# A transposed input in two halves of the tokens for the opening stage of a two-layer attention encoder

## The chip, the cores and the metric

The kernel runs on one core of one Trainium2 chip. The metric is the device time of one execution in microseconds; the profile comes from one profiled execution on the chip. Times of instructions are read from its trace.

## What is computed

A two-layer encoder over 1024 tokens of 1024 features, in float32. Each layer normalises x, scales and shifts it feature by feature (the modulation, computed from a vector c by a product with `ada_w`), projects it, runs attention and adds the gated result to x. Layer 0 joins latent attention (queries and keys go through narrow latents of 384 and 256 features, each with a norm of its own) with stick-breaking attention; layer 1 is differential attention. The change concerns the start of layer 0 as far as the latents `cq` and `ckv`.

```python
def rms_norm(x, g, eps=NORM_EPS):
    xf = x.astype(jnp.float32)
    y = xf * lax.rsqrt(jnp.mean(xf * xf, axis=-1, keepdims=True) + eps)
    return (y * g.astype(jnp.float32)).astype(x.dtype)
...
def layer_ab(h, pos, w_in, q_norm_g, kv_norm_g, w_uq, w_ukv, w_out):
    B, S, _ = h.shape
    proj = h @ w_in
    cuts = np.cumsum([MLA_Q_LORA, MLA_KV_LORA, MLA_ROPE, SB_W, SB_W, SB_W]).tolist()
    cq, ckv, kr, q_sb, k_sb, v_sb, z = jnp.split(proj, cuts, axis=-1)
    q = (rms_norm(cq, q_norm_g) @ w_uq).reshape(B, S, MLA_HEADS, MLA_NOPE + MLA_ROPE)
    ...
    kv = (rms_norm(ckv, kv_norm_g) @ w_ukv).reshape(B, S, MLA_HEADS, MLA_NOPE + MLA_V)
    ...
    o_mla = mla_attention(q, k, kv[..., MLA_NOPE:]).reshape(B, S, MLA_HEADS * MLA_V)
    o_sb = stick_breaking_attention(q_sb.reshape(shp), k_sb.reshape(shp), v_sb.reshape(shp)).reshape(B, S, SB_W)
    y = jnp.concatenate([o_mla, o_sb], axis=-1) * jax.nn.silu(z)
    return y @ w_out
...
    c_act = jax.nn.silu(c)
    for i in range(DEPTH):
        mod = c_act @ ada_w[i] + ada_b[i]
        shift, scale, gate = jnp.split(mod, 3, axis=-1)
        h = rms_norm(x, norm_g[i]) * (1.0 + scale[:, None, :]) + shift[:, None, :]
        ...
        x = x + gate[:, None, :] * out
    return rms_norm(x, final_g)
```

## The kernel before

Every matrix product is done as three: each operand is split into a high part, rounded to 12 bits, and an exact rest, and `mm3` (lines 172 to 175) adds high x high, high x low and low x high into one PSUM bank. A block of weights is 128 columns wide; `wprep` (line 164) loads it into the tile `w_st`, ScalarE casts the high part and VectorE or GpSimd subtracts the rest (`split`, `sub`, lines 153 to 162). `dense_fm` (line 177) multiplies one block with the 8 feature blocks of the tokens, in two halves of 512 tokens, 24 products each.

The order of work is that of a scheduler: instructions are written in a program order, it places them on the engines when its model finds them ready, and every engine then runs its own list in that order. SP's list holds all DMA issues. Tiles with one tag share a fixed number of slots, so a tile can wait for the release of another.

The opening (lines 496 to 728) makes the modulated, transposed tokens hT: 8 feature blocks of 128 rows by 1024 tokens, as high and low parts (`h0h`, `h0l`). x comes in 8 tiles of 128 tokens by 1024 features. ScalarE or VectorE square and sum each row (lines 523 and 526), `rstd_cols` (line 188) makes the inverse root in thirteen small VectorE instructions, and each tile is scaled in one pass (lines 532, 534). For feature block k, `ada_block` (line 538) computes shift and scale: eight VectorE instructions over a 1 MB tile of `ada_k` (lines 542 and 544, tile `ack`), sums over partitions on TensorE (line 547), two tiny instructions (lines 548, 549). Then TensorE transposes the eight 128 x 128 pieces of x (line 554), and `modulate` (line 237) lets ScalarE scale and shift a bank of four into `hf` and cast the high part, while GpSimd or VectorE subtracts the low one.

The first three latent blocks run feature by feature as hT comes, for all tokens, in six PSUM banks; the fourth and fifth follow whole. `latent` (line 612) evacuates each bank with a square on ScalarE (line 620), a cast times a gain (line 621) and a subtraction on VectorE (line 622), stores both parts to DRAM for later, and makes the norm of the three query blocks and of the two key blocks by column sums (`row_sums`, line 230). Behind them come the relative position rows, the rotary tables, the rotated shared key (block 21), four blocks of the gate z, and, by `more` (line 606), in pieces queued behind the last x subtraction (`ready`) and the last store of the first three latents (`behind`), the modulation sweeps for layer 1 and the gates (`ada_sweep`, line 472). Then the stick-breaking heads begin.

## Time and profile before

| | |
|---|---|
| Median of 3 runs | 1491.65 us (1491.1 to 1492.06) |
| Span of the profiled execution | 1489.6 us |
| TensorE products busy | 1394.9 us, 94% of the span |
| VectorE busy | 956.8 us, 64% |
| ScalarE busy | 670.5 us, 45% |
| GpSimd busy | 446.2 us, 30% |

Busy shares are averages over stages. The profile gives them in forty slices too, and the trace can be asked for a stretch, for one engine in order of time, or for groups of instructions by line. A row in order of time has the start, the duration, the engine, the line and the operation with its output and inputs; several equal instructions in a row are merged (x4). In square brackets stands the idle time before it and what released it. A product's duration overlaps with the next one's, so the spacing of starts tells its cost.

### The profile page before, as it was taken

Reading aid. Unit: us, or ns where it says so; the run is one execution under the profiler, and the core shown is the slowest. Engines: PE = TensorE matmul, PEld = TensorE weight load, DVE = VectorE, ACT = ScalarE, POOL = GpSimd, SP = SyncE. Lnnn points to the kernel's source line nnn. Section 1 sums busy time; section 2 is a strip of 40 time slices with the busy share of each in tenths; the row PEclk is TensorE's granted clock in tenths of the full one; section 3 lists DMA queues with packets and bytes.
Section 4 is the critical chain, followed back from the end, with each engine's and each line's share of the span. In section 5 each row is a group of like instructions: output and inputs, shape, how many; then the busy total and the mean of one; then the engine's idle time right before and its main releaser. Section 6 shows DMA issues by size and latency. Waiting matters only on the chain.

```text
span 1489.6 us, 20993 instructions
## 1 busy us (share of the span) xinstructions
PE 1394.9 (94%) x7328; PEld 1160.7 (78%) x7328; DVE 956.8 (64%) x2155; ACT 670.5 (45%) x1368; POOL 446.2 (30%) x509
## 2 busy tenths in 40 slices
PE   3899999999998899999879899999999999997797
...
GB/s 375 67 261 382 206 77 75 49 90 50 75 69 186 36 188 213 136 123 100 215 136 268 29 108 48 86 85 114 71 100 64 92 64 114 78 111 179 82 201 93
DMA packets 109640, 189.85 MB, mean 127 GB/s; under 512 B 8736, under 2 KB 70040, under 8 KB 107488
## 3 DMA queue, kind: packets, MB, share of 16 engines
...
## 4 chain that ended last, share of the span: by engine, by line
PE 40%; DVE 5%; DMA 4%; issue 1%; POOL 1%; ACT 1%; SPq 0%; DVEq 0%; ACTq 0%; POOLq 0%
PE psd L173 8%; PE psd L175 8%; PE psd L174 8%; PE sc L294 4%; PE pv L328 3%; PE sc L173 2%; PE sc L174 2%; PE sc L175 2%; DMA y_hi<-yh_d 1%; DMA w_st<-in_wo_dram 1%; PE pv L234 1%; PE tr L308 1%; PE tr L309 1%; PE tr L310 1%; DVE g L1029 1%
## 5 line engine op out<-in xcount | busy, mean ns | idle before, releaser
L154 POOL TENSOR_TENSOR w_lo<-w_st,w_hi 128x1024 fp32r<-128x1024 f32 (+2 forms) x63 | 153.6, 2440 | 370.7 <-ACT w_hi L159 370.4
L154 DVE TENSOR_TENSOR pt_l<-tr,pt_h 128x512 fp32r<-128x512 f32 (+1 forms) x240 | 148.8, 630 | 104.9 <-ACT pt_h L159 97.4
L159 ACT CAST pt_h<-tr 128x512 fp32r<-128x512 f32 (+1 forms) x240 | 126.2, 547 | 147.0 <-PE tr L310 136.1
L175 PE MATMUL psd<-h1h,w_lo 128*128 128x512 f32 x448 | 177.0, 395 | 0.0
L174 PE MATMUL psd<-h1l,w_hi 128*128 128x512 f32 x448 | 176.2, 393 | 0.0
L173 PE MATMUL psd<-h1h,w_hi 128*128 128x512 f32 x448 | 176.1, 393 | 0.0
L294 PE MATMUL sc<-qk_k,qk_a 128*128 128x512 f32 (+2 forms) x288 | 104.8, 369 | 3.6 <-ACT g L747 1.3
L173 PE MATMUL psd<-h0h,w_hi 128*128 128x512 f32 x264 | 106.7, 404 | 0.0
L174 PE MATMUL psd<-h0l,w_hi 128*128 128x512 f32 x264 | 105.6, 400 | 0.0
L175 PE MATMUL psd<-h0h,w_lo 128*128 128x512 f32 x264 | 105.2, 398 | 0.0
L294 PE MATMUL sc<-qk_k,qk_b 128*128 128x512 f32 (+2 forms) x288 | 98.5, 349 | 0.0
L1029 DVE CUSTOM_DVE_ANT_0 g<-sc,tz 128x512 f32<-128x512 f32 (+3 forms) x128 | 72.1, 585 | 40.1 <-PE sc L294 33.7
L159 ACT CAST w_hi<-w_st 128x1024 fp32r<-128x1024 f32 x56 | 58.9, 1052 | 86.4 <-PE sc L174 36.2
L174 PEld LDWEIGHTS psd<-h1l,w_hi 128*128 128x128 f32 x448 | 84.2, 188 | 17.1
L175 PEld LDWEIGHTS psd<-h1h,w_lo 128*128 128x128 f32 x448 | 84.2, 188 | 16.1
L173 PEld LDWEIGHTS psd<-h1h,w_hi 128*128 128x128 f32 x448 | 84.2, 188 | 16.1
L328 PE MATMUL pv<-pt_l,vt 128*128 128x256 f32 x320 | 88.7, 303 | 8.2 <-DVE pt_l L154 7.4
L1035 ACT ACTIVATE g<-g,st 128x640 f32<-128x640 f32 (+3 forms) x64 | 63.4, 990 | 67.8 <-DVE st L1034 63.1
L328 PE MATMUL pv<-pt_h,vt 128*128 128x256 f32 x320 | 89.5, 296 | 3.3 <-POOL pt_h L314 1.7
L749 DVE TENSOR_TENSOR_SCAN g<-g 128x640 f32<-128x640 f32 (+3 forms) x32 | 68.7, 2148 | 14.7 <-ACT g L746 14.6
L328 PEld LDWEIGHTS pv<-pt_l,vt 128*128 128x128 f32 x320 | 62.0, 194 | 12.0 <-issue 4.7
L328 PEld LDWEIGHTS pv<-pt_h,vt 128*128 128x128 f32 x320 | 61.8, 193 | 9.5 <-DVE ot L418 2.7
...
## 6 DMA issues: line engine op xcount, KB each, us to landing
...
```

The source lines that it names most:

```text
L154: return (nc.vector if eng == "vec" else nc.gpsimd).tensor_tensor(out_, x_, y_, op=ALU.subtract)
L159: nc.scalar.copy(hi, src)
L173: mm(ps, sh, mh, start=start, stop=False)
L174: mm(ps, sh, ml, start=False, stop=False)
L175: mm(ps, sl, mh, start=False, stop=stop)
L234: mm(ps[:, t:t + 1], tile_of(t), ones, start=True, stop=True)
L294: mm(ps[:, :nn], st[:, q], mv[:, lo_:lo_ + nn], start=m == 0, stop=not diag and m == len(pairs) - 1)
L308: nc.tensor.transpose(tr[:, P:256], pb[:, (2 * j + 1) * P:(2 * j + 2) * P], identf)
L328: mm(dst, st, tt[w][:, m * 256:m * 256 + 256], start=j == 0 and m == 0 and x == 0, stop=j == n - 1 and m == 1 and x == len(ps_) - 1)
L749: nc.vector.tensor_tensor_scan(ur, ur, ur, 1.0, op0=ALU.mult, op1=ALU.bypass)
L1029: nc.vector.tensor_tensor_reduce(e_[:, sl], ps, tz[:, S - L + sl.start:S - L + sl.stop], op0=ALU.add, op1=ALU.max, scale=1.0, scalar=-3e38 ...
L1035: nc.scalar.activation(e_[:, :L], e_[:, :L], AF.Exp, scale=0.125, bias=st[:, 2 + c:3 + c], accum_out=lst[:, c1:c1 + 1] if c == 0 else st[: ...
```

## The change

x is handed over transposed and cut into two halves of 512 tokens (`xt`: for each half four tiles with two feature blocks each). `x_norm` squares the eight feature blocks of a half on ScalarE, adds them up (VectorE for the first half, GpSimd for the second), takes column sums on TensorE, the inverse root, and spreads it over the partitions by four scaled identities and products (`cols_bc`) into a tile `rbx`. `x_mod` multiplies a feature block by it, lets ScalarE scale, shift and cast it, and subtracts the low part; the multiplication and the subtraction are VectorE's for features 0 and 1 of the first half and for even features of the second, GpSimd's otherwise. The transposes of x go. Five latent blocks instead of three run feature by feature, on the first half alone, in five banks; then their banks are evacuated in half-width tiles, the second half is normalised and modulated, and the five blocks run on it one after the other. The norms of the latents follow at the end. All five split weights stay on the chip meanwhile. Feature block 0 of the modulation is summed by TensorE instead of VectorE; the first two weight blocks have their low parts from VectorE, the others from GpSimd. `ready` is now the last subtraction of the second half, `behind` the last store of all five latents.

The diff, without removed comments and docstrings and without renamed tiles further down:

```diff
-SC = "avavavvv"
-LOK = lambda k, g: k in (0, 7)
-WLO = ("vec", "pool")
+WLO = ("vec", "vec", "pool", "pool", "pool")
...
-    X_TAGS = [("lsq0", 1), ("lsq1", 1), ("lsq2", 1), ("zb", 2), ("zb", 2), ("lat_h", 2), ("lat_h", 2), ("lat_l", 2)]
...
         def ada_load(k):
             ada_st[k] = a0.tile([P, KC, 256], F32, name="ada_st", tag="ld", bufs=NLD)
             dma(ada_st[k].rearrange("p r c -> p (r c)"), a["ada_k"][k])
-            return ada_st[k]
-        xts = []
-        junka = a0.tile([P, 2, D], F32, name="junka", tag="acc")
-        for g in range(2):
-            ss = a0.tile([P, 4], F32, name="ss", tag="ss", bufs=2)
+        def wide(name, tag):
+            return a0.tile([P, S], F32, name=name, tag=tag, bufs=4)
+        def x_load(half):
+            ts = []
             for j in range(4):
-                t = 4 * g + j
-                tag, bufs = X_TAGS[t]
-                xt = a0.tile([P, D], F32, name="xt", tag=tag, bufs=bufs)
-                dma(xt, a["x"][t * P:t * P + P, :])
-                if j % 2:
-                    junk = a0.tile([P, D], F32, name="junk", tag="junk")
-                    nc.vector.tensor_tensor_reduce(junk, xt, xt, op0=ALU.mult, op1=ALU.add, scale=1.0, scalar=0.0,
-                                                   accum_out=ss[:, j:j + 1])
-                else:
-                    nc.scalar.activation(junka[:, 0, :], xt, AF.Square, accum_out=ss[:, j:j + 1])
-                xts.append(xt)
-            rs = rstd_cols(a0, ss, 4, 1.0 / D, 1e-6, "rc")
-            for j in range(4):
-                xt = xts[4 * g + j]
-                if SC[4 * g + j] == "a":
-                    nc.scalar.activation(xt, xt, AF.Copy, scale=rs[:, j:j + 1])
-                else:
-                    nc.vector.tensor_scalar(xt, xt, rs[:, j:j + 1], None, op0=ALU.mult)
-            if g == 0:
-                ada_load(0)
+                t_ = wide("xt", "ab"[half])
+                dma(t_, a["xt"][half, j])
+                ts.append(t_)
+            return [ts[k // 2][:, k % 2 * 512:k % 2 * 512 + 512] for k in range(KC)]
+        def x_norm(half, xk):
+            add = nc.vector if half == 0 else nc.gpsimd
+            acc = a0.tile([P, 512], F32, name="sqa", tag="sqa", bufs=1)
+            for k in range(KC):
+                sq = acc if k == 0 else a0.tile([P, 512], F32, name="sq", tag="hf", bufs=2)
+                nc.scalar.activation(sq, xk[k], AF.Square)
+                if k:
+                    add.tensor_tensor(acc, acc, sq, op=ALU.add)
+            ss = row_sums(lambda t: acc[:, t * P:t * P + P], 4, v_bank)
+            r = rstd_cols(a0, ss, 4, 1.0 / D, 1e-6, "rc")
+            bc = cols_bc(acc, r, v_bank)
+            rb = a0.tile([P, 512], F32, name="rbx", tag="rbx", bufs=1)
+            nc.vector.tensor_copy(rb, bc)
+            return rb
         def ada_block(k):
-            st = ada_st[k] if k in ada_st else ada_load(k)
-            ac = a0.tile([P, 256], F32, name="ack", tag="ack", bufs=2)
-            nc.vector.tensor_scalar(ac, st[:, 0, :], c_act[:, 0:1], None, op0=ALU.mult)
-            for r in range(1, KC):
-                nc.vector.scalar_tensor_tensor(ac, st[:, r, :], c_act[:, r:r + 1], ac, op0=ALU.mult, op1=ALU.add)
+            st = ada_st[k]
             ps = t_bank()
-            for n in range(2):
-                mm(ps[:, n:n + 1], ac[:, n * P:n * P + P], ones, start=True, stop=True)
+            if k == 0:
+                for n in range(2):
+                    for r in range(KC):
+                        mm(ps[:, n:n + 1], st[:, r, n * P:n * P + P], c_act[:, r:r + 1], start=r == 0, stop=r == KC - 1)
+            else:
+                ac = a0.tile([P, 256], F32, name="ack", tag="ack", bufs=2)
+                nc.vector.tensor_scalar(ac, st[:, 0, :], c_act[:, 0:1], None, op0=ALU.mult)
+                for r in range(1, KC):
+                    nc.vector.scalar_tensor_tensor(ac, st[:, r, :], c_act[:, r:r + 1], ac, op0=ALU.mult, op1=ALU.add)
+                for n in range(2):
+                    mm(ps[:, n:n + 1], ac[:, n * P:n * P + P], ones, start=True, stop=True)
             nc.vector.tensor_tensor(modc[0][:, k::8], ps[:, 0:2], adab[:, k:16:8], op=ALU.add)
             nc.vector.scalar_tensor_tensor(gsc[0][:, k:k + 1], modc[0][:, 8 + k:9 + k], 1.0, ng[:, k:k + 1],
                                            op0=ALU.add, op1=ALU.mult)
-            for g in range(2):
-                tr = t_bank()
-                for j in range(4):
-                    nc.tensor.transpose(tr[:, j * P:(j + 1) * P], xts[4 * g + j][:, k * P:(k + 1) * P], identf)
-                last = modulate(a0, hT, 0, k, slice(g * 512, g * 512 + 512), tr, "act", "vec" if LOK(k, g) else "pool")
-            return last
+        def x_mod(half, k, xk, rb):
+            sl = slice(half * 512, half * 512 + 512)
+            vec = (k < 2) if half == 0 else (k % 2 == 0)
+            (nc.vector if vec else nc.gpsimd).tensor_tensor(xk, xk, rb, op=ALU.mult)
+            nc.scalar.activation(xk, xk, AF.Identity, scale=gsc[0][:, k:k + 1], bias=modc[0][:, k:k + 1])
+            return split(hT[k][0][:, sl], hT[k][1][:, sl], xk, "act", "vec" if vec else "pool")
+        in_a0 = lambda tag, bufs: (lambda t_: (lambda name: t_[:, 0 if name == "w_hi" else 1, :]))(
+            a0.tile([P, 2, 1024], F32R, name="wl", tag=tag, bufs=bufs))
+        def w_load(b):
+            alloc = None if b < 2 else in_a0("acc", 1) if b == 2 else in_a0("ld", NLD)
+            return wprep(a["w0"][16 + b], eng_lo=WLO[b], alloc=alloc)
+        x0 = x_load(0)
+        ada_load(0)
+        wl = [w_load(0), w_load(1)]
+        rb0 = x_norm(0, x0)
         ada_block(0)
-        wq3 = [wprep(a["w0"][16 + b], eng_lo=WLO[b]) for b in range(2)]
-        w3 = a0.tile([P, 2, 1024], F32R, name="w3", tag="acc")
-        wq3.append(wprep(a["w0"][18], alloc=lambda name: w3[:, 0 if name == "w_hi" else 1, :]))
-        first = [[s_bank(), s_bank()], [s_bank(), d_bank()], [d_bank(), v_bank()]]
+        wl.append(w_load(2))
+        ada_load(1)
+        wl += [w_load(3), w_load(4)]
+        for k in (2, 3):
+            ada_load(k)
+        wlk = [tuple(t_.rearrange("p (k c) -> p k c", c=P) for t_ in w) for w in wl]
+        fb = [s_bank(), s_bank(), s_bank(), d_bank(), d_bank()]
+        x_mod(0, 0, x0[0], rb0)
         for k in range(KC):
             if k + 1 < KC:
-                ready = ada_block(k + 1)
-            for b in range(3):
-                wh, wl = (t.rearrange("p (k c) -> p k c", c=P) for t in wq3[b])
-                for half in range(2):
-                    sl = slice(half * 512, half * 512 + 512)
-                    mm3(first[b][half], wh[:, k, :], wl[:, k, :], hT[k][0][:, sl], hT[k][1][:, sl], k == 0, k == KC - 1)
-        w4 = a0.tile([P, 2, 1024], F32R, name="w4", tag="ld", bufs=NLD)
-        wk = [wprep(a["w0"][19], alloc=lambda name: w4[:, 0 if name == "w_hi" else 1, :])]
+                ada_block(k + 1)
+                x_mod(0, k + 1, x0[k + 1], rb0)
+                if k + 4 < KC:
+                    ada_load(k + 4)
+            if k == 0:
+                x1 = x_load(1)
+            for b in range(5):
+                mm3(fb[b], wlk[b][0][:, k, :], wlk[b][1][:, k, :], hT[k][0][:, :512], hT[k][1][:, :512], k == 0, k == KC - 1)
+        sqt = {}
+        def latent_evac(b, half, ps):
+            sl = slice(half * 512, half * 512 + 512)
+            if b % 2 == 0:
+                sqt[half, b // 2] = wide("lsq", "ab"[half])
+            gain, hi_d, lo_d, j = (qg, cqh_d, cql_d, b) if b < 3 else (kvg, ckh_d, ckl_d, b - 3)
+            nc.scalar.activation(sqt[half, b // 2][:, b % 2 * 512:b % 2 * 512 + 512], ps, AF.Square)
+            lh = a0.tile([P, 512], F32R, name="lat_h", tag="lat_h", bufs=2)
+            ll = a0.tile([P, 512], F32R, name="lat_l", tag="lat_l", bufs=2)
+            nc.scalar.activation(lh, ps, AF.Copy, scale=gain[:, j:j + 1])
+            nc.vector.scalar_tensor_tensor(ll, ps, gain[:, j:j + 1], lh.bitcast(F32), op0=ALU.mult, op1=ALU.subtract)
+            dma(hi_d[j][:, sl], lh)
+            return dma(lo_d[j][:, sl], ll)
+        for b in range(5):
+            latent_evac(b, 0, fb[b])
+        rb1 = x_norm(1, x1)
+        for k in range(KC):
+            ready = x_mod(1, k, x1[k], rb1)
+        for b in range(5):
+            ps = (s_bank, d_bank)[b % 2]()
+            for k in range(KC):
+                mm3(ps, wlk[b][0][:, k, :], wlk[b][1][:, k, :], hT[k][0][:, 512:], hT[k][1][:, 512:], k == 0, k == KC - 1)
+            behind = latent_evac(b, 1, ps)
...
-        def latent(nblk, w_first, gain, hi_d, lo_d, row_d, banks=None):
-            tags = [("lsq0", 1), ("lsq1", 1), ("lsq2", 1)] if banks else [("zb", 2)] * 2
-            sq = [a0.tile([P, S], F32, name="lsq", tag=tag, bufs=bufs) for tag, bufs in tags]
-            for b in range(nblk):
-                lh = a0.tile([P, S], F32R, name="lat_h", tag="lat_h", bufs=2)
-                ll = a0.tile([P, S], F32R, name="lat_l", tag="lat_l", bufs=2)
-                def evac(ps, half, sl):
-                    nc.scalar.activation(sq[b][:, sl], ps, AF.Square)
-                    nc.scalar.activation(lh[:, sl], ps, AF.Copy, scale=gain[:, b:b + 1])
-                    nc.vector.scalar_tensor_tensor(ll[:, sl], ps, gain[:, b:b + 1], lh[:, sl].bitcast(F32),
-                                                   op0=ALU.mult, op1=ALU.subtract)
-                if banks:
-                    for half in range(2):
-                        evac(banks[b][half], half, slice(half * 512, half * 512 + 512))
-                else:
-                    dense_fm(wk.pop() if wk else wprep(a["w0"][w_first + b]), hT, evac, s_bank)
-                dma(hi_d[b], lh)
-                stored = dma(lo_d[b], ll)
-            for x_ in sq[1:]:
-                nc.gpsimd.tensor_tensor(sq[0], sq[0], x_, op=ALU.add)
-            ss = row_sums(lambda t: sq[0][:, t * P:t * P + P], NT, v_bank)
-            r = rstd_cols(a0, ss, NT, 1.0 / (nblk * P), 1e-6, "rl")
+        def latent_norm(b0, n, row_d):
+            part = lambda half, b: sqt[half, b // 2][:, b % 2 * 512:b % 2 * 512 + 512]
+            for half in range(2):
+                for b in range(b0 + 1, b0 + n):
+                    nc.gpsimd.tensor_tensor(part(half, b0), part(half, b0), part(half, b), op=ALU.add)
+            ss = row_sums(lambda t: part(t // 4, b0)[:, t % 4 * P:t % 4 * P + P], NT, v_bank)
+            r = rstd_cols(a0, ss, NT, 1.0 / (n * P), 1e-6, "rl")
             row_out(a0, r, NT, row_d, v_bank)
-            return stored
-        krt = a0.tile([P, S], F32, name="krt", tag="lat_h", bufs=2)
+        krt = wide("krt", "b")
...
-        behind = latent(3, 16, qg, cqh_d, cql_d, rq_d, first)
+        latent_norm(0, 3, rq_d)
+        latent_norm(3, 2, rkv_d)
...
-        rqb = a0.tile([P, S], F32, name="rqb", tag="lsq2", bufs=1)
+        rqb = wide("rqb", "b")
         dma(rqb, row_bc(rq_d, P))
-        latent(2, 19, kvg, ckh_d, ckl_d, rkv_d)
         more(3)
-        te = a0.tile([P, S], F32, name="te", tag="lsq0")
+        te = wide("te", "a")
         nc.vector.tensor_copy(te[0:64], rqb[0:64])
         nc.vector.tensor_mul(te[64:128], rqb[64:128], cs[64:128])
         dma(tq_d[0], te)
-        to = a0.tile([P, S], F32, name="to", tag="lsq1")
+        to = wide("to", "a")
         nc.vector.tensor_mul(to[0:64], rqb[0:64], cs[0:64])
         nc.vector.tensor_copy(to[64:128], rqb[64:128])
         dma(tq_d[1], to)
...
-        "x": f["x"][0], "pos": f["pos_offset"].reshape(1, 1), "tab": f["rel_bias_table"],
+        "x": f["x"][0], "xt": f["x"][0].T.reshape(4, 2, P, 2, 512).transpose(3, 0, 2, 1, 4).reshape(2, 4, P, 1024),
+        "pos": f["pos_offset"].reshape(1, 1), "tab": f["rel_bias_table"],
```

## Rows read from the trace of the kernel before

**Rows 1.** The page's busy tenths of TensorE, forty slices of 37.2 us.
```profile
PE   3899999999998899999879899999999999997797
```

**Rows 2.** Stretches: PE, PEld, DVE, ACT, POOL busy us (instructions), clock, DMA share, GB/s.
```profile
40.00:45.00 5.00, 1.34 (x6) 0.75 (x4) 5.00 (x4) 1.87 (x3) 5.00 (x3) 0.88 0.01 5
...
50.00:60.00 10.00, 10.00 (x51) 8.30 (x50) 9.09 (x13) 3.95 (x7) 5.30 (x4) 0.97 0.34 107
...
70.00:80.00 10.00, 10.00 (x53) 8.04 (x51) 3.74 (x9) 6.24 (x10) 2.57 (x2) 1.00 0.06 14
```

**Rows 3.** TensorE in order of time, 25 to 52 us: start us, us, engine, line, what.
```profile
25.18 0.80 PE L173 MATMUL sc<-h0h,w_hi 128*128 128x512 f32 x1 [4.00 <-ACT h0h L159]
...
45.88 0.98 PE L547 MATMUL tr<-ones_sq,ack 128*128 128x1 f32 x4 [4.54 <-DVE ack L544]
...
49.32 0.63 PE L174 MATMUL sc<-h0l,w_hi 128*128 128x512 f32 x1
...
49.74 0.63 PE L175 MATMUL sc<-h0h,w_lo 128*128 128x512 f32 x1
...
51.75 0.40 PE L173 MATMUL psd<-h0h,w 128*128 128x512 f32 x1
...
51.98 0.40 PE L174 MATMUL psd<-h0l,w 128*128 128x512 f32 x1
```

**Rows 4.** TensorE in order of time, 80 to 109 us.
```profile
80.07 0.81 PE L585 MATMUL tr<-oh,tab 32*8 32x384 f32 x2
...
99.25 1.84 PE L234 MATMUL pv<-ones_sq,lsq 128*128 128x1 f32 x16
...
108.56 0.39 PE L175 MATMUL sc<-h0h,w_lo 128*128 128x512 f32 x1
```

**Rows 5.** VectorE in order of time, 27 to 60 us.
```profile
27.93 0.35 DVE L542 TENSOR_SCALAR ack<-ada_st,c_act 128x256 f32<-128x256 f32 x1
...
28.19 0.88 DVE L544 SCALAR_TENSOR_TENSOR ack<-ada_st,c_act,ack 128x256 f32<-128x256 f32 x2
...
28.98 0.68 DVE L154 TENSOR_TENSOR h0l<-hf,h0h 128x512 fp32r<-128x512 f32 x1
...
29.58 4.56 DVE L544 SCALAR_TENSOR_TENSOR ack<-ada_st,c_act,ack 128x256 f32<-128x256 f32 x11
...
38.02 9.14 DVE L544 SCALAR_TENSOR_TENSOR ack<-ada_st,c_act,ack 128x256 f32<-128x256 f32 x9
...
55.76 3.61 DVE L544 SCALAR_TENSOR_TENSOR ack<-ada_st,c_act,ack 128x256 f32<-128x256 f32 x7
```

**Rows 6.** GpSimd in order of time, 36 to 63 us.
```profile
36.68 2.65 POOL L154 TENSOR_TENSOR h0l<-hf,h0h 128x512 fp32r<-128x512 f32 x2 [13.37 <-ACT h0h L159]
...
42.54 2.52 POOL L154 TENSOR_TENSOR w<-w_st,w 128x1024 fp32r<-128x1024 f32 x1
...
52.21 2.90 POOL L154 TENSOR_TENSOR h0l<-hf,h0h 128x512 fp32r<-128x512 f32 x2
...
59.80 2.53 POOL L154 TENSOR_TENSOR h0l<-hf,h0h 128x512 fp32r<-128x512 f32 x2 [4.70 <-ACT h0h L159]
```

**Rows 7.** TensorE in order of time: a transpose of x.
```profile
57.09 1.04 PE L554 MATMUL tr<-identf,xt 128*128 128x128 f32 x8
```

**Rows 8.** VectorE in order of time: its square of the fourth x tile.
```profile
9.12 1.23 DVE L523 CUSTOM_DVE_ANT_0 junk<-xt 128x1024 f32<-128x1024 f32 x1 [1.43 <-DMA xt<-in_x_dram]
```

**Rows 9.** ScalarE by line and form, 0 to 250 us: count | busy us, mean ns | idle before.
```profile
L239 ACT ACTIVATE hf<-tr,modc,gsc 128x512 f32<-128x512 f32 x16 | 12.2, 777 | 33.4 <-DVE gsc L549 20.9 <-PE tr L554 10.8 <-POOL h0l L154 1.7
...
L159 ACT CAST h0h<-hf 128x512 fp32r<-128x512 f32 x16 | 9.7, 622 | 0.3
```

**Rows 10.** VectorE in order of time: the first and last of thirteen root steps.
```profile
140.02 0.15 DVE L192 TENSOR_SCALAR rlh<-pv 128x8 f32<-128x8 f32 x1
...
142.22 0.17 DVE L203 SCALAR_TENSOR_TENSOR rlr<-rlt,rlr 128x8 f32<-128x8 f32 x1
```

**Rows 11.** SP's queue in order of time: the first issues of the later modulation.
```profile
93.65 10.02 SPq L80 DMA_DIRECT2D ada_st<-in_ada_w_dram  x10
```

6 lines of the change are left out of this document (3 added, 3 removed).

## Prediction

> **What bounds the kernel now.** I began with the busy shares in forty slices: TensorE stands at eight or nine tenths nearly everywhere, and at three in the first slice of 37 us [rows 1]. So a change in the opening is worth what it does to the moment from which TensorE no longer starves, plus or minus the TensorE work behind it. The table of stretches gives that moment: from 40 to 45 us TensorE is busy for 1.34 us of 5, from 50 us on it is busy all the time [rows 2]. The order of TensorE's instructions says the same: the first product of the latent blocks starts at 25.18, there is a wait of 4.54 us before 45.88 with DVE's accumulation (`ack`) as the releaser, and from 51.75 products start every 0.23 us [rows 3]. The last of the 240 products of the five latent blocks starts at 108.56 and so ends at about 109.0 us; sixteen row sums of the queries' norm and the small table products lie ahead of it [rows 4]. I take **109.0 us** as the mark: whatever the change does to it, the saturated work behind it moves with it.
>
> What starves TensorE is not DMA, which is idle from 40 to 45 us (5 GB/s) [rows 2]. It is VectorE and GpSimd together. Alone, VectorE runs eleven accumulations in 4.56 us, 0.407 us each; beside GpSimd nine take 9.14 us [rows 5], and GpSimd at that time runs one subtraction after another [rows 6]. To see whether the two exclude each other I added up the 31.4 us from 27.93 to 59.37, in which VectorE is never idle: 41 accumulations of 0.407 (16.7), five first steps of 0.26 (1.3), one subtraction of 0.60, eight tiny instructions (0.9), and on GpSimd six half-width subtractions of 1.27 and two full ones of 2.45 (12.5) [rows 5, 6]. That is 32.0 us of work in 31.4 us. So in this stage instructions of the two engines on on-chip tiles add up as if they ran on one engine; I call it the shared budget.
>
> The Trainium skill states the same in "SBUF — State Buffer", section "SBUF: two separate sides": VectorE instructions with two SBUF inputs, or in a two-port mode, and GpSimd's exclude each other for a whole instruction; it speaks against the change. It leaves out instructions with one input in PSUM, such as the `lat_l` subtraction. No run here separates those; if they counted, the first half's five would add an estimated 3.8 us to the sum below, and by the page they add nothing.
>
> **The change, part by part.**
>
> *x arrives transposed, the 64 transposes go.* Eight transposes take some 0.8 us at the fast spacing [rows 7]; 36 of the 64 lie after 50 us, where TensorE is the limit, so about 3.5 us of its work goes there. The rest lay in starved time and is worth nothing. The loads stay eight of 512 KB on the same queue: no change.
>
> *Start.* The fourth x tile is in at 9.1 us [rows 8], and it is now all that the first half needs. Then: two squares on ScalarE, 1.2 (by the 0.62 us of a 512-column pass [rows 9]); one addition, 0.6 (the spacing of a 512-column subtraction [rows 5]); four column sums on a slow TensorE, 1.0 (the row at 45.88 [rows 3]); thirteen small instructions for the root, 2.4 [rows 10]; spreading the columns over the partitions, which the trace of before does not show: at least four small steps, 0.8, at most 2.0 with four products between them, I take 1.5 as the steps pipeline; a copy, 0.6. That is 16.4 us; one weight subtraction (1.2) falls into it, so **17.5 us**. The scaling, the affine pass (0.78) and the cast (0.62) [rows 9] put the first product near 20, five microseconds before the old one. That alone brings nothing if the stage behind it is slower.
>
> *The shared budget from 17.5 us until the second half can begin.* VectorE: seven accumulation blocks (block 0 goes to TensorE, where it runs in idle time) of 0.26 + 7 x 0.407 = 3.11, 21.8 us; scaling and subtraction of features 0 and 1, 4 x 0.60 = 2.4. GpSimd: the low halves of three weight blocks, 3 x 2.45 = 7.4; scaling and subtraction of six features, 12 x 1.27 = 15.2; the seven additions of the second half's norm, 8.9. Sum 55.7, so it is through at **73.2 us**. Before, the normalisation was one pass over the wide tile by ScalarE or VectorE; now every feature block pays a multiplication by the row of norms, most of them on the slower engine. Within this budget the order hardly matters: additions early delay the accumulations, additions late delay the second half.
>
> *TensorE meanwhile.* Five blocks on one half are 15 products a feature: 3.5 us at 0.23, 6.3 at 0.42 [rows 3]. The budget gives a feature about every 7 us, so TensorE keeps up at either clock and is idle for about half of the stage. The first half ends near 76 us.
>
> *The change of halves.* The second half's norm goes through column sums, root, spreading and copy once more and then scaling, affine pass and cast: 1.0 + 2.4 + 1.5 + 0.6 + 0.6 + 0.8 + 0.6 = 7.5, so the first product of the second half starts at **80.7 us**. Nothing else is ready for TensorE but the table products. Its 120 products take 27.6 us. The idle time ahead of them resembles the 4.54 us before 45.88, after which products were 0.42 us apart until about 50 us, the 1.2 GHz level [rows 3]; that costs ten products 0.19 us each, 1.9. Two things can hold up the second half's features: ScalarE has 8 x 1.4 us for them and stands behind the first half's evacuation, which now has two half-width `lat_h` tiles that wait for their stores; and their share of the budget is 15 us for eight, 1.9 us each, against 3.5 us that five interleaved blocks or 0.7 us that a single block needs. That is 0 to 4 us; I take 1.5. The sixteen row sums, 1.7 [rows 4]. Together 80.7 + 27.6 + 1.9 + 1.5 + 1.7 = 113.4, and 1.0 for table products and row sums that do not fit into idle time: **114.4 us against 109.0, 5.4 us later**.
>
> *Behind the mark.* `more` queues the sixteen tiles of layer 1's modulation on SP behind the last latent store; before, that is 93.65 [rows 11], because three blocks were through early; now it follows all five, near 115. Half of the latent stores have left by then, on an idle DMA. The sums over partitions of these sweeps stand in TensorE's order among the z blocks; I take the delay at zero, covered by three to four blocks of products (11 us each), and 8 us if the cover is gone. The key norm, now beside the query norm, costs what it did.
>
> Sum: profiled span 1489.6 + 5.4 = 1495.0. The median of the runs lies 2.05 us above the span, so **1497 us**.
>
> **Rivals.**
> 1. *The forecast*: a slower opening by the shared budget, 1493 to 1502: 0.47.
> 2. *Ideal interleaving.* The second half's norm and first features are worked off within the first half, so that products run on without a hole: first half through at 73.2 + 3.5 = 76.7, second at 104.3, row sums 106.0, 3.0 us earlier: 1488.7. For it: the budget is the same in any order. Against it: GpSimd has to pass 23 us of work that stands earlier in the program, and the hole at the change of halves is a chain of small steps. Up to 1493 it is no measurable change: 0.22.
> 3. *The budget is only partly shared* (faster). If half of GpSimd's 31.5 us runs beside VectorE, the budget ends at 57.5, the second half starts at 65 and the mark is at 98.7: 10 us earlier, 1481. With none of it shared GpSimd's 31.5 us alone set the stage, 49.0 us, and the mark is at 90.2: 1473. It decides from 10 us of overlap on. For it: VectorE's instructions of this stage with a PSUM input, and tiny ones, may pass. Against it: the 32.0 in 31.4 us. 0.18, most of it at the near end.
> 4. *The modulation of layer 1 comes late.* The second sweep's sums hold TensorE: another 8 us, 1505. For it: they start 20 us later while TensorE is only 5 later. Against it: half of the latent stores no longer compete with them for DMA. 0.13.
>
> That the transposes are not really gone, or x is loaded twice, the diff excludes.
>
> **How the numbers follow.** A measurement of this kernel tells about 0.2%, 3 us, from no change. The predicted time is that of the first case. Faster by more than that: case 3 and the best part of case 2, 0.23. Within: the rest of case 2 and the near edge of case 1, 0.22. Slower: 0.55. The range for eight in ten runs from 1482, the near end of case 3, to 1506, case 4; it leaves out a budget that is not shared at all and a double delay.
>
> **What would show it.** Right: no transposes of x; the first product near 20 us; VectorE's accumulations slow (1 us and more) wherever GpSimd is busy, between 18 and 70 us; TensorE about half idle until 75 us; a hole of some 5 us before the first product on the second half near 81 us, at the low clock behind it; the last latent product near 113. Wrong: accumulations of 0.4 us beside a busy GpSimd, a last feature of the first half before 60 us, or a mark before 105 us. If the mark is where I put it but the end is not, the loss or gain lies in the modulation sweeps or in the clock of the z blocks.

## The result and the profile after

The changed kernel takes 1528.96 us (median of 4 runs, 1526.02 to 1533.41) against 1491.86 us (4 runs, 1491.1 to 1492.73) on the same chip: 2.5% slower, ratio 1.0247, 95% interval 1.0225 to 1.0268. The forecast had the sign and not the size: 5.4 us later were forecast, 37.1 came. The profiled execution spans 1526.9 us against 1489.6, 37.3 more.

The page after, busy tenths of TensorE and its granted clock in forty slices of 38.2 us; TensorE answers to [rows 1]:

```profile
PE   4689799999999889999888899999999999998897
...
PEclk9689799999999999999999999999999999998899
```

The weak stretch no longer ends with the first slice: slices two and three (38 to 115 us) stand at 6 and 8, the fifth (153 to 191 us) at 7, where before there were eights and nines. So two stages lost time. The table of stretches after (TensorE, its weight loads, VectorE, ScalarE, GpSimd busy us; clock; DMA share; GB/s), against [rows 2]:

```profile
30.00:40.00 10.00, 5.21 (x17) 3.33 (x16) 1.21 (x1) 1.74 (x3) 10.00 (x7) 0.89 0.16 48
...
50.00:60.00 10.00, 5.13 (x17) 4.40 (x18) 9.93 (x33) 1.43 (x2) 1.30 (x1) 0.50 0.98 368
...
70.00:80.00 10.00, 4.34 (x10) 3.13 (x10) 10.00 (x14) 6.83 (x11) 8.12 (x5) 0.66 0.00 1
80.00:90.00 10.00, 4.50 (x13) 3.75 (x14) 7.95 (x16) 4.69 (x9) 2.67 (x2) 0.60 0.00 0
...
150.00:160.00 10.00, 3.11 (x13) 2.23 (x12) 10.00 (x21) 0.00 (x0) 10.00 (x1) 0.86 0.99 401
...
180.00:190.00 10.00, 7.16 (x21) 5.75 (x22) 9.96 (x17) 0.00 (x0) 0.00 (x0) 0.66 0.93 385
```

From 30 to 40 us VectorE works 1.21 us of 10 and GpSimd all 10; from 70 to 80 us both are busy (10.00 and 8.12), from 80 to 90 us still VectorE (7.95), and TensorE works less than half of the time at a granted clock of 0.66 and 0.60; from 150 to 160 us both are busy all the time and TensorE works 3.11 us.

To size the two stages I use two marks. The first is the prediction's: the end of the last latent product with the sixteen row sums of the queries' norm. The second is ScalarE's first cast of the stick-breaking stage. TensorE after, in order of time (answering to [rows 4]), then that cast before and after:

```profile
131.56 0.40 PE L173 MATMUL sc<-h0h,wl 128*128 128x512 f32 x1
131.80 1.84 PE L232 MATMUL pv<-ones_sq,lsq 128*128 128x1 f32 x16
133.50 0.47 PE L171 MATMUL sc<-h0h,w_hi 128*128 128x512 f32 x1
```

```profile
L159 ACT CAST qk_a<-psd x5: 576/587/634, 187.0 to 245.9; 128x512 fp32r<-128x512 f32 x5
```

```profile
L157 ACT CAST qk_a<-psd x3: 576/586/587, 223.4 to 247.3; 128x512 fp32r<-128x512 f32 x3
```

| stage | before | after | difference |
|---|---|---|---|
| to the mark | 109.0 | 133.5 | +24.5 |
| mark to first cast | 78.0 | 89.9 | +11.9 |
| rest of the span | 1302.6 | 1303.5 | +0.9 |

**The opening.** SP's queue, then VectorE, GpSimd and TensorE after, in order of time:

```profile
15.87 24.11 SPq L78 DMA_DIRECT2D w_st<-in_w_dram  x4
40.03 2.00 SPq L78 DMA_DIRECT2D ada_st<-in_ada_k_dram  x4
```

```profile
22.28 0.69 DVE L532 COPY rbx<-pv 128x512 f32<-128x512 f32 x1 [0.32 <-PE pv L225]
...
23.28 3.43 DVE L558 TENSOR_TENSOR xt<-xt,rbx 128x512 f32<-128x512 f32 x2
...
46.43 0.84 DVE L545 TENSOR_SCALAR ack<-ada_st,c_act 128x256 f32<-128x256 f32 x1 [15.03 <-DMA ada_st<-in_ada_k_dram]
...
68.50 6.79 DVE L558 TENSOR_TENSOR xt<-xt,rbx 128x512 f32<-128x512 f32 x4
...
87.43 0.48 DVE L547 SCALAR_TENSOR_TENSOR ack<-ada_st,c_act,ack 128x256 f32<-128x256 f32 x1
...
93.18 0.16 DVE L550 TENSOR_TENSOR modc<-tr,smalls 128x2 f32<-128x2 f32 x1 [5.19 <-PE tr L549]
```

```profile
24.45 9.33 POOL L558 TENSOR_TENSOR xt<-xt,rbx 128x512 f32<-128x512 f32 x6
33.74 1.26 POOL L527 TENSOR_TENSOR sqa<-sqa,sq 128x512 f32<-128x512 f32 x1
34.96 4.67 POOL L152 TENSOR_TENSOR wl<-w_st,wl 128x1024 fp32r<-128x1024 f32 x2
...
44.48 3.98 POOL L527 TENSOR_TENSOR sqa<-sqa,sq 128x512 f32<-128x512 f32 x3
...
66.84 6.23 POOL L558 TENSOR_TENSOR xt<-xt,rbx 128x512 f32<-128x512 f32 x4 [2.67 <-DVE rbx L532]
```

```profile
13.36 6.96 PE L542 MATMUL tr<-c_act,ada_st 128*128 128x1 f32 x32
20.19 2.05 PE L225 MATMUL pv<-sqa,ones_sq 128*128 128x128 f32 x8
...
26.97 1.22 PE L171 MATMUL sc<-h0h,w_hi 128*128 128x512 f32 x2 [2.53 <-ACT h0h L157]
...
74.80 0.79 PE L172 MATMUL sc<-h0l,w_hi 128*128 128x512 f32 x1 [5.50 <-POOL h0l L152]
85.50 0.98 PE L549 MATMUL tr<-ones_sq,ack 128*128 128x1 f32 x4 [6.37 <-DVE ack L547]
103.93 0.50 PE L171 MATMUL sc<-h0h,w_hi 128*128 128x512 f32 x1 [1.01 <-DVE lat_l L605]
```

SP's queue stands from 15.87 to 40.0 us at four weight tiles: the staging tile `w_st` has two buffers, and one is freed only by GpSimd's low half at 34.96, behind six multiplications and two additions. Modulation tiles 2 to 5 stand behind them in the queue, so VectorE is idle for 15.03 us, while GpSimd works without a pause (22.99 to 48.46). Afterwards the two engines hold each other up: a multiplication that takes 0.6 us alone (e6 below) takes 1.7 (6.79 for four). These four and GpSimd's four at 66.84 are the second half's, and they stand in the lists ahead of what the first half's last features still need. The second half's first product starts at 103.93, with hardly a wait.

**Behind the mark.** TensorE, GpSimd and VectorE after (the first step of a norm's root, the first sweep steps, ten more):

```profile
158.96 0.79 PE L171 MATMUL sc<-h0h,w_hi 128*128 128x512 f32 x1 [6.89 <-DVE krt L668]
182.84 0.80 PE L171 MATMUL sc<-h0h,w_hi 128*128 128x512 f32 x1 [4.97 <-DVE zb L249]
```

```profile
145.81 14.72 POOL L152 TENSOR_TENSOR w_lo<-w_st,w_hi 128x1024 fp32r<-128x1024 f32 x1 [11.80 <-ACT w_hi L157]
167.97 2.35 POOL L152 TENSOR_TENSOR w_lo<-w_st,w_hi 128x1024 fp32r<-128x1024 f32 x1
```

```profile
133.93 0.15 DVE L190 TENSOR_SCALAR rlh<-pv 128x8 f32<-128x8 f32 x1
...
139.62 0.88 DVE L476 TENSOR_SCALAR acc<-ada_st,c_act 128x512 f32<-128x512 f32 x2 [3.31 <-DMA ada_st<-in_ada_w_dram]
...
143.80 6.69 DVE L478 SCALAR_TENSOR_TENSOR acc<-ada_st,c_act,acc 128x512 f32<-128x512 f32 x10
```

VectorE before, the same two first steps, and TensorE's wait for `krt` from mark to first cast (us in total, times, longest):

```profile
101.29 0.16 DVE L192 TENSOR_SCALAR rlh<-pv 128x8 f32<-128x8 f32 x1
102.13 0.88 DVE L478 TENSOR_SCALAR acc<-ada_st,c_act 128x512 f32<-128x512 f32 x2 [0.69 <-DMA ada_st<-in_ada_w_dram]
```

```profile
PE sc L173 <- DVE krt L642: 0.4, 1, 0.4
```

TensorE waits for a bank that VectorE empties (`krt`, `zb`), while VectorE runs sweep steps that stand ahead in its list; GpSimd's low half of a weight block takes 14.72 us instead of 2.35. Before, TensorE waits 0.4 us for `krt` and not for `zb`.

### The profile page after: what moved, and what is told of

Same layout as the page of the kernel before. It is cut to its first block, busy times and chain, and to the rows that moved or that the text cites. A ratio compares the mean times of both kernels' runs of the same rounds, so it can differ in the third digit from the quotient of the medians.

```text
span 1526.9 us, 21035 instructions
## 1 busy us (share of the span) xinstructions
PE 1408.9 (92%) x7324; PEld 1172.6 (77%) x7324; DVE 955.9 (63%) x2160; ACT 672.6 (44%) x1373; POOL 475.1 (31%) x526
## 4 chain that ended last, share of the span: by engine, by line
PE 37%; DMA 6%; DVE 4%; ACT 2%; POOL 1%; issue 1%; SPq 0%; DVEq 0%; ACTq 0%; POOLq 0%
PE psd L171 7%; PE psd L172 7%; PE psd L173 7%; PE sc L292 4%; PE pv L326 3%; PE sc L171 2%; PE sc L172 1%; PE sc L173 1%; DMA rb<-rst_d 1%; DMA y_hi<-yh_d 1%; PE pv L232 1%; DMA qk_k<-qk_a 1%; PE tr L306 1%; DMA tz<-rel_d 1%; PE tr L307 1%
## 5 line engine op out<-in xcount | busy, mean ns | idle before, releaser
L152 POOL TENSOR_TENSOR w_lo<-w_st,w_hi 128x1024 fp32r<-128x1024 f32 (+2 forms) x61 | 158.3, 2597 | 346.3 <-ACT w_hi L157 345.9
L326 PE MATMUL pv<-pt_l,vt 128*128 128x256 f32 x320 | 90.1, 306 | 8.2 <-DVE pt_l L152 7.4
L173 PEld LDWEIGHTS psd<-h1h,w_lo 128*128 128x128 f32 x448 | 84.2, 188 | 16.1
L775 DVE TENSOR_TENSOR_SCAN g<-g 128x640 f32<-128x640 f32 (+3 forms) x32 | 68.8, 2148 | 14.7 <-ACT g L772 14.5
```

The source lines that it names most:

```text
L152: return (nc.vector if eng == "vec" else nc.gpsimd).tensor_tensor(out_, x_, y_, op=ALU.subtract)
L173: mm(ps, sl, mh, start=False, stop=stop)
L326: mm(dst, st, tt[w][:, m * 256:m * 256 + 256], start=j == 0 and m == 0 and x == 0, stop=j == n - 1 and m == 1 and x == len(ps_) - 1)
L775: nc.vector.tensor_tensor_scan(ur, ur, ur, 1.0, op0=ALU.mult, op1=ALU.bypass)
```

## The experiments

All were run beside the kernel before, whose median was 1487.9 to 1491.3 us. The columns "mark" and "first cast" are from each profiled execution, as above. A mark is thus one reading: the six runs with the opening of the changed kernel (after, e3, e7, e9, e13, e16) put it at 131.7 to 133.5 us, the six with e11's (e11, e12, e14, e15, e17, e18) at 109.5 to 113.5. Medians of rows that were not run together carry the spread of the kernel before as well, up to 4 us.

| run | median us (lowest to highest) | mark | first cast | between |
|---|---|---|---|---|
| before | 1491.9 | 109.0 | 187.0 | 78.0 |
| after | 1529.0 | 133.5 | 223.4 | 89.9 |
| e1 tiles first | 1525.8 (1524.4 to 1528.8) | 130.8 | 220.8 | 90.1 |
| e2 low halves on VectorE | 1523.0 (1520.8 to 1528.7) | 128.5 | 218.2 | 89.7 |
| e3 sweeps early | 1527.5 (1524.4 to 1530.2) | 133.5 | 224.8 | 91.3 |
| e4 e1 and e3 | 1529.7 (1527.6 to 1532.9) | 129.5 | 221.4 | 91.9 |
| e5 no GpSimd | 1506.9 (1505.4 to 1509.8) | 117.4 | 207.7 | 90.3 |
| e6 all on VectorE | 1507.1 (1505.5 to 1511.1) | 114.1 | 204.2 | 90.1 |
| e11 first half first | 1502.2 (1499.2 to 1505.7) | 110.9 | 200.4 | 89.5 |
| e7 after, sweeps cut | 1520.8 (1515.1 to 1524.9) | 132.5 | 211.9 | 79.4 |
| e8 before, sweeps cut | 1485.4 (1482.0 to 1488.1) | 110.0 | 182.6 | 72.6 |
| e9 banks by ScalarE | 1516.8 (1513.7 to 1529.5) | 132.8 | 216.9 | 84.1 |
| e10 before, late sweeps | 1494.5 (1490.7 to 1499.6) | 107.9 | 190.1 | 82.2 |
| e12 e11 and e9 | 1499.5 (1487.2 to 1509.2) | 112.5 | 207.3 | 94.8 |
| e13 sweeps in step | 1520.4 (1517.1 to 1521.8) | 131.7 | 218.2 | 86.5 |
| e16 in step, early | 1526.4 (1524.0 to 1529.7) | 131.8 | 220.0 | 88.2 |
| e14 e11 and e13 | 1500.8 (1495.5 to 1503.7) | 109.5 | 196.2 | 86.7 |
| e15 and low halves | 1496.5 (1491.6 to 1502.8) | 113.5 | 197.1 | 83.6 |
| e17 e11 and e16 | 1496.3 (1493.5 to 1498.5) | 110.2 | 193.2 | 83.0 |
| e18 e17 and low halves | 1491.4 (1487.3 to 1493.6) | 110.9 | 189.8 | 78.9 |

### The opening: the queue, or the budget?

**e1**, all eight modulation tiles ahead of the last three weight blocks.
```diff
-        wl.append(w_load(2))
         ada_load(1)
-        wl += [w_load(3), w_load(4)]
         for k in (2, 3):
             ada_load(k)
+        wl += [w_load(2), w_load(3), w_load(4)]
```


> The changed kernel with the loads of modulation tiles 1 to 3 written ahead of the weight blocks 2 to 4, nothing else. Theory Q (the queue): in the changed kernel SP's list has four weight loads that wait for a staging tile (one row of 24.11 us from 15.87) ahead of the modulation tiles 2 to 5, VectorE has nothing to accumulate from 31.4 to 46.4 us, and TensorE starves for it. With the tiles loaded first VectorE works on from 23 us, the last latent product comes 12 to 20 us earlier than 132 and the end with it: 1509 to 1517 us. Theory S (the shared budget of the prediction alone): the accumulations are late because GpSimd's multiplications and additions hold VectorE off, so the order of loads matters little: 1525 to 1529 us, and the accumulations are merely spread out.

1525.8 us, inside the second theory's window: the waiting queue is not the bound. VectorE hardly idles any more and is through with its accumulations 14.3 us earlier (73.6 instead of 87.9 us), but the second half's multiplications now come after that, and what the first half gains (its last product ends at 92.4 instead of 102.9 us) is lost at the change of halves. The mark is 2.7 us earlier. VectorE, then TensorE in order of time, e1:

```profile
73.10 0.47 DVE L547 SCALAR_TENSOR_TENSOR ack<-ada_st,c_act,ack 128x256 f32<-128x256 f32 x1
...
76.68 5.74 DVE L558 TENSOR_TENSOR xt<-xt,rbx 128x512 f32<-128x512 f32 x4
```

```profile
83.60 0.79 PE L172 MATMUL sc<-h0l,w_hi 128*128 128x512 f32 x1 [4.03 <-POOL h0l L152]
...
99.36 0.80 PE L171 MATMUL sc<-h0h,w_hi 128*128 128x512 f32 x1 [6.92 <-DVE lat_l L604]
```

**e2**, the low halves of all five latent weight blocks on VectorE.
```diff
-WLO = ("vec", "vec", "pool", "pool", "pool")
+WLO = ("vec",) * 5
```


> The changed kernel with the low halves of all five weight blocks on VectorE instead of three of them on GpSimd; SP's list is the same up to the latents. Theory Q: the staging tiles come free as soon as ScalarE has cast (about 30 us) instead of after GpSimd's six multiplications (39.6 us), so the modulation tiles are issued some 8 us earlier: 1517 to 1523 us. Theory S: only 3 x (2.45 - 1.22) = 3.7 us of budget go: 1524 to 1527 us.

1523.0 us, mark 5.0 us earlier. Three instructions of 2.45 us became three of 1.2 [rows 5, 6], 3.8 us less of shared work; the time lies at the border of the two windows (0.04 us inside the first) and does not separate the theories alone.

**e3**, the sweeps gated by the first half's last latent store, and **e4**, e1 and e3 together.
```diff
-            latent_evac(b, 0, fb[b])
+            behind = latent_evac(b, 0, fb[b])
...
-            behind = latent_evac(b, 1, ps)
+            latent_evac(b, 1, ps)
```


> The changed kernel with the sweeps of layer 1's modulation queued behind the first half's last latent store instead of the second half's. Theory L (late sweeps): between the last latent product and the stick-breaking heads the changed kernel loses another 12 us, because the sweeps start 40 us later than before, VectorE is filled with them when the key rotation and the z blocks need it, and TensorE waits 6.9 and 5.0 us; with the sweeps 20 us earlier that goes: 1515 to 1521 us. Rival C (collision): GpSimd's weight subtraction and VectorE's sweeps exclude each other wherever they meet, moving the sweeps only moves the wait: 1526 to 1531 us.

> Both edits: modulation tiles of layer 0 loaded ahead of the weight blocks, sweeps of layer 1 queued behind the first half's store. If the two losses are separate they add: 1497 to 1506 us, which is the shared budget of the prediction alone. If the first edit brings the latents forward so far that the sweeps no longer come late, the second adds nothing to the first (within 3 us of it).

1527.5 and 1529.7 us (1527.6 to 1532.9): no gain. In e3 the sweeps start 20 us earlier (first tile issued at 114.6 instead of 134.4 us) and the wait for `krt` grows from 6.9 to 10.1 us. Starting them earlier in the same order does not help.

**e5**, with e1's loads, nothing of the opening on GpSimd: its multiplications left out, its low halves copies on ScalarE, its additions on VectorE.
```diff
-            (nc.vector if vec else nc.gpsimd).tensor_tensor(xk, xk, rb, op=ALU.mult)
+            if vec:
+                nc.vector.tensor_tensor(xk, xk, rb, op=ALU.mult)
```


> The changed kernel with all eight modulation tiles loaded ahead of the last three latent weight blocks (as in the run that only reordered the loads, 1525.75 us, last latent product near 129 us), and in the opening nothing is left on GpSimd up to the second half's last feature: the multiplications by the row of norms that stood there are left out, the low halves that stood there become plain copies on ScalarE, the additions of the second half's norm move to VectorE. So the scaling of ten of the sixteen feature halves and the low halves of three weight blocks and ten feature halves are left out of the result. VectorE keeps its own list. Theory S (GpSimd's work and what it does to VectorE's accumulations set the opening): VectorE's own work is 21.8 us of accumulations, 4.9 of scaling and subtractions, 4.2 of additions, from 23 us on, so the second half can begin near 60 us and the last latent product ends between 86 and 95 us; the run comes to 1482 to 1493 us. Rival T (the queue of loads, ScalarE's passes or TensorE's waits on banks set it): accumulations at 0.4 us, but the last latent product still later than 115 us, run 1510 us or more.

1506.9 us: between the two windows. The mark comes 13.4 us earlier than in e1, but the extra copies load ScalarE: it was busy all of 30 to 40 us, and TensorE waited 7.0 us in all for its casts and 5.6 us at the change of halves. That ScalarE is now the bound is argued from these waits. The run shows that leaving GpSimd's share out was worth 13 us here, not what it would be worth without the copies.

**e6**, everything of the opening on VectorE, e1's loads.
```diff
-            vec = (k < 2) if half == 0 else (k % 2 == 0)
+            vec = True
...
-            add = nc.vector if half == 0 else nc.gpsimd
+            add = nc.vector
```
(and e2's edit)

> The same base (modulation tiles loaded first, 1525.75 us), with every multiplication, low half and addition of the opening on VectorE; nothing of the computation is left out. Theory S (the two engines take turns): GpSimd's 31.5 us of work become some 17 us on VectorE (0.6 us where GpSimd takes 1.27, 1.2 where it takes 2.45), so the last latent product comes 10 to 18 us earlier than in that run and the time is 1505 to 1516 us. Rival P (the two engines had mostly worked side by side and the sum was mis-read): VectorE's list gets 17 us longer without anything in return, 1530 to 1545 us.

1507.1 us, mark 16.7 us earlier than in e1, both inside the first theory's window: giving all of GpSimd's work to VectorE is worth 16.7 us at the mark and 18.7 by the medians (15.6 by the two ratios to the kernel before beside them, 1.0240 and 1.0135). VectorE in order of time, e6, six of the same multiplications as above:

```profile
24.11 3.69 DVE L558 TENSOR_TENSOR xt<-xt,rbx 128x512 f32<-128x512 f32 x6
```

0.6 us each, against 1.7 beside GpSimd. GpSimd as a helper cost more than it took over.

**e11**, e6 with the second half's multiplications issued behind the first half's last feature (`done0`).
```diff
-                x_mod(0, k + 1, x0[k + 1], rb0)
+                done0 = x_mod(0, k + 1, x0[k + 1], rb0)
...
         rb1 = x_norm(1, x1)
-        for k in range(KC):
-            ready = x_mod(1, k, x1[k], rb1)
+        with tc.issue_after(done0.ins):
+            for k in range(KC):
+                ready = x_mod(1, k, x1[k], rb1)
```


> The run with the whole opening on VectorE (1507.1 us) with one more edit: the second half's multiplications by its norm row and what follows them are issued behind the last feature of the first half. The amount of work stays the same. In that run VectorE was never idle from 20 to 70 us, and some 12 us of second-half work stood ahead of the last two modulation tiles, so that the first half ended at 81 us and the last latent product at 112.4. Theory O (the order inside the budget sets the end, against the step of the prediction that the order hardly matters): first half through near 66 to 70 us, the last latent product at 97 to 104 us, the run 1492 to 1500 us. Rival A (the amount alone counts; what the first half gains a hole at the change of halves takes back): within 4 us of 1507.

1502.2 us, 4.9 less and outside both windows: the order counts, but less than I expected. The first half ends at 77.4 instead of 83.6 us. Of these 6.2 us 1.5 are lost at the change of halves (a wait of 2.55 us instead of 1.01) and 1.5 within the second half. Both theories were too simple: amount and order matter, and the change of halves takes back part of each gain. The 3.2 us that are left at the mark are no larger than the spread of this opening over its six runs (109.5 to 113.5), in which 110.9 is the middle. The mark is now 1.9 us behind the kernel before.

### Behind the mark: 12 us

In every run up to here the time from mark to first cast stays at 89.5 to 91.9 us (89.5 to 90.3 where the sweeps were not moved), wherever the mark lies. So this part hardly depends on the opening.

**e7 and e8**, the sweeps' multiply-adds cut to 16 columns, in the kernel after and in the kernel before.
```diff
-  scalar_tensor_tensor(a_, s_, c_act[:, kk:kk + 1], a_, ...)
+  scalar_tensor_tensor(a_[:, :16], s_[:, :16], c_act[:, kk:kk + 1], a_[:, :16], ...)
```


> The changed kernel as it is, but in the sweeps of the modulation of layer 1 and of the gates the seven multiply-adds of each quarter work on 16 columns instead of 512 (the loads stay, the sums are wrong). To be set against the same cut in the kernel before. Theory C (behind the mark the loss of 12 us is the sweeps of VectorE that now fall among block 21 and the z blocks): the two cut kernels differ by 22 to 27 us, the shift of the last latent product alone; the waits of TensorE for krt and zb between 150 and 185 us are gone. Rival D (the loss is in the loads themselves, DMA being at 400 GB/s there, or in the order of the queue): they differ by 33 to 39 us as the uncut kernels do.

> The kernel before with the same cut in the sweeps (seven multiply-adds of each quarter on 16 columns, the sums are wrong). In the kernel before these sweeps hardly hold TensorE (busy 118.4 of the 120 us from 110 to 230), so both theories expect the same of it: 1484 to 1491 us against 1489 to 1492.

1520.8 and 1485.4 us, 35.4 apart: by the time that is my rival. By the marks it is half of each: 79.4 against 72.6 us, 6.8 of the 11.9 are left. So VectorE's sweep arithmetic makes about half, as far as one profiled execution of each can say (another 3.9 us of their difference lie behind the first cast); the theory that it makes all fell. Nor are all waits gone, as it had expected: TensorE still waits 4.6 us for `krt`.

**e10**, one part alone: the kernel before, sweeps gated by the fifth latent block's store.
```diff
-        behind = latent(3, 16, qg, cqh_d, cql_d, rq_d, first)
+        latent(3, 16, qg, cqh_d, cql_d, rq_d, first)
...
-        latent(2, 19, kvg, ckh_d, ckl_d, rkv_d)
+        behind = latent(2, 19, kvg, ckh_d, ckl_d, rkv_d)
```


> The kernel before with one part of the change alone: the sixteen tiles of the sweeps are queued behind the last store of the fifth latent block instead of the third, as in the changed kernel. In the list that results, the first krt multiplication stands ahead of all sweep instructions and the second behind six of them, where the changed kernel has 24 ahead of both. Theory E (it is the place of the bank-freeing instructions in VectorE's list that costs, not the lateness of the sweeps): a small loss, 1490 to 1496 us. Rival L (a sweep that begins 25 us later is itself late for its sums on TensorE or fights with other loads): 1498 to 1506 us, most of the 12 us.

1494.5 us, ratio 1.0029 (1.0012 to 1.0046), 82.2 us from mark to cast: late sweeps alone cost 4 us, by the median and from mark to cast, here by one wait of 6.90 us for `zb`. (The profiled execution is one of the fastest and wins 3.0 us back behind the cast.) The other 8 need the changed kernel.

**e9**, banks of block 21 and the z blocks emptied by ScalarE (the same for `zb`).
```diff
-            nc.vector.tensor_mul(krt[:, sl], ps, cs[:, sl])
+            nc.scalar.copy(krt[:, sl], ps)
+            nc.vector.tensor_mul(krt[:, sl], krt[:, sl], cs[:, sl])
```


> The changed kernel as it is, but the products of block 21 and of the four z blocks are copied out of their banks by ScalarE, and VectorE multiplies the copies; the order of the sweeps in VectorE's list stays (24 multiply-adds and some tiny steps of the key norm stand ahead of the krt multiplications). Theory E (behind the mark TensorE loses its 12 us because banks are freed by VectorE instructions that stand in its list behind sweep instructions, which are paced by their loads and by VectorE's own time): the waits of 6.9 us on krt and 5.0 us on zb go, with some of the low clock behind them; 1513 to 1519 us against 1526 to 1529. Rival W (the low halves of the z weights, 14.7 us on a GpSimd that gets no turn beside the sweeps, end last in any case): the waits move to w_lo and the run stays within 5 us, 1521 to 1529 us.

1516.8 us, inside the first window, and 5.8 us less between mark and cast. The waits for `krt` and `zb` are gone, others came in their place. TensorE and VectorE, e9:

```profile
159.88 2.72 PE L485 MATMUL tr<-ones_sq,acc 128*128 128x1 f32 x12 [2.85 <-DVE acc L478]
169.07 0.37 PE L207 MATMUL pv<-identf,rlr 128*8 128x128 f32 x1 [6.47 <-DVE rlr L201]
```

```profile
161.82 2.30 DVE L201 SCALAR_TENSOR_TENSOR rlr<-rlt,rlr 128x8 f32<-128x8 f32 x1
```

The key norm's root, thirteen tiny steps, stands between sweep steps in VectorE's list (last step at 168.8 us; the three before it took 2.30, 2.27 and 2.27 us), and TensorE's list holds its transpose ahead of the next products.

**e13**, each group of sweep tiles issued behind the multiplication that empties the last block's bank (the same gate is set in the z blocks).
```diff
-                nc.vector.tensor_mul(krt[:, sl], ps, cs[:, sl])
+                gate[0] = nc.vector.tensor_mul(krt[:, sl], ps, cs[:, sl])
...
-            with tc.issue_after(ready.ins), tc.issue_after(behind.ins):
+            with tc.issue_after(gate[0].ins), tc.issue_after(behind.ins):
```


> The changed kernel as it is, but each group of sweep tiles is issued behind the multiplication that frees the bank of the block just computed (krt, then each z block), so that at most 12 sweep multiply-adds stand ahead of krt in VectorE's list (24 in the changed kernel) and the root of the key norm comes ahead of krt without sweep steps between. The work and the loads are the same. Theory E (the 12 us behind the mark are the place of the instructions that free banks, and of the low halves beside them, against the sweeps): from the last latent product to the first cast of the stick-breaking stage 80 to 85 us instead of 91.6 (78 in the kernel before), 1515 to 1521 us. Rival V (too little room: 42 us of sweep multiply-adds have to fit behind the mark into a stage of about 78 us whatever their order): within 4 us of the changed kernel, 1524 to 1530 us.

1520.4 us, inside the first window, but only 3.4 us less from mark to cast. The expectations of e13 and e16 count from the last latent product, 1.7 us ahead of the mark of the table: by that measure e13 has 88.2 us where the first theory wanted 80 to 85, and e16 89.9 where it wanted 78 to 82. Both are misses. TensorE's two longest waits, e13, from mark to first cast (us in total, times, longest):

```profile
PE sc L171 <- DVE zb L731: 8.6, 1, 8.6
PE sc L171 <- DVE krt L670: 1.0, 1, 1.0
```

The wait moved on from `krt` to the first z block, behind fifteen sweep steps (10 us from 152.43 on) and the four instructions of `te` and `to` (8 us).

**e16**, e13 with the first six sweep tiles behind the first half's stores (e3's edit, `more(6)` for `more(3)`).

> The changed kernel with the sweeps in step as in the run that only did this (1520.4 us, where the wait moved to the first z block's multiplication, 8.6 us), and the first six sweep tiles issued behind the first half's latent stores, some 25 us before the last latent product, where VectorE was busy for 2 to 3 us of 10. Theory V (room: behind the last latent product 42 us of sweep steps do not fit among 55 us of block 21 and z blocks without holding the bank-freeing steps; the kernel before had 23 us of them done or under way by its last latent product plus ten): 1507 to 1514 us, from the last latent product to the stick-breaking stage 78 to 82 us. Rival (the tiles now compete with the latent stores and the z weights on the one queue, so that the last latent or block 21 comes late): 1517 to 1524 us.

1526.4 us, outside both windows: my theory of room fell, and its rival's range with it. The waits for banks are down to 1.0 us, but the sums of the sweep (4.9) and the norm's root (2.6) now hold TensorE.

### Both stages mended

**e12**: e11 and e9. **e14**: e11 and e13. **e15**: e14 with the low halves of block 21 and the z weights on VectorE (`eng_lo="vec"`). **e17** and **e18**: e14 and e15 with e16's early tiles.

> That run and the copies out of the banks by ScalarE together; nothing is left out. If the opening and the stage behind it add up: the gain of the order (7 to 15 us) and of the banks (8 to 13 us) on 1507.1, so 1480 to 1491 us, as fast as the kernel before or faster. If the wait behind the mark only moves to the z weights' low halves: 1492 to 1500 us.

> The opening wholly on VectorE with the first half first (1502.2 us), and the sweeps in step as in the run before this one. Theory E: the two gains add, 1490 to 1496 us. Rival V: 1499 to 1504 us.

> As the run before it, and the low halves of block 21 and of the z weights, which took GpSimd 14 to 19 us beside the sweeps, are made by VectorE (1.2 us each, in its list between the sweep steps). If the turn-taking with GpSimd is the rest of the loss behind the mark: another 2 to 5 us, 1486 to 1493 us, level with the kernel before (1488 to 1492). If the list of VectorE is the bound there: the same or up to 4 us slower than the run before it.

> The same two edits of the sweeps on the opening that is wholly on VectorE with the first half first (1500.8 us with the sweeps in step alone). Theory V: 1486 to 1493 us, level with the kernel before (1488 to 1492). Rival: 1496 to 1503 us.

> That run with the low halves of block 21 and of the z weights on VectorE as well (1496.5 us without the early sweeps). Theory V: 1484 to 1491 us. Rival: 1493 to 1499 us.

e12 is inconclusive: 1499.5 us lies in its second window, but ten executions of it lie between 1487.2 and 1509.2, and the profiled one is the slowest, with 94.8 us from mark to cast where e9, the same edit there, had 84.1. e14 and e17 fell into the windows of their rivals (1500.8 and 1496.3 us); e15 missed both of its windows (1496.5 us, twelve runs from 1491.6 to 1502.8), though it is 4.3 us faster than e14. e18 is 0.4 us above the upper edge of its window: 1491.4 us, ratio 1.0009 (0.9997 to 1.0022), level with the kernel before. Its 78.9 us from mark to cast are near the 78.0 of before. From e14 to e15 and from e17 to e18 the only edit is the low halves, and it is worth 3.1 and 4.1 us from mark to cast. So the changed opening can be as fast as the old one; none of these versions is faster.

## Why the prediction was wrong

**What bounds the opening: right.** VectorE and GpSimd share one budget also here. From 46.43 to 87.9 us VectorE is hardly idle; at the prediction's prices its instructions there come to 28.0 us (42 accumulations, six first steps, four multiplications, three subtractions, the rest small) and GpSimd's to 16.1 (seven subtractions, four multiplications, 2.1 of additions): 44.1 us of work in 41.5 elapsed, so all but some 3 us of it took turns. The trace agrees, within these 3 us, with the rule quoted from the Trainium skill ("SBUF — State Buffer", section "SBUF: two separate sides"). e6 says the same: with GpSimd's work on VectorE the mark came 16.7 us earlier.

**Start, 17.5 us: 5.5 too early.** The row of norms was ready at 22.97. Two weight subtractions fell into the root, not one, and accumulations of block 1; the spreading took eight products and 2.05 us on TensorE alone, where I had 1.5 us for steps and products together; and it stood behind the modulation of block 0, which holds TensorE for 6.96 us from 13.36 on and which I had put into idle time.

**"The loads stay eight of 512 KB on the same queue: no change": wrong, but worth little at the mark.** I counted bytes and not the order of the queue. Four weight loads stood ahead of modulation tiles 2 to 5, with two staging buffers that are freed by GpSimd, to which I had myself given 23 us of other work, and VectorE waited 15.03 us. But GpSimd used the budget meanwhile, and e1, which took the wait away, moved the mark by 2.7 us.

**"Within this budget the order hardly matters", 55.7 us and the first half done near 76: the step that failed in the opening.** The 55.7 us hold the first half's features and the second half's additions, and the sum lets the second half's features follow. The lists did not keep to that. Between 22.97 and 87.9, where VectorE is through with its accumulations, the instructions of both engines come to an estimated 69 us at the same prices, in 65 elapsed. Against the 55.7 these are 13 us more: eight multiplications and six subtractions of the second half (13.1) and some 5 of small instructions, less some 5 of the first half that were done before or came after. With the 5.5 of the start, and 4 that ran side by side, that is the whole delay: 87.9 instead of 73.2 us, 14.7 later. In e1 the first half's accumulations went first and were through at 73.6, near the forecast, and the second half's work stood behind them instead: the amount is the same, and so nearly is the mark. e11 changed nothing but the order, on e6's amount, and gained 3.2 at the mark, within the spread of single marks.

| | forecast | after | e1 |
|---|---|---|---|
| row of norms ready | 17.5 | 23.0 | 23.6 |
| accumulations through | 73.2 | 87.9 | 73.6 |
| first half's last product ends | 76 | 102.9 | 92.4 |
| second half's first product | 80.7 | 103.9 | 99.4 |
| mark | 114.4 | 133.5 | 130.8 |

**From there to the end of the first half: 15.0 us, forecast 2.8 (in e1 18.8).** The last features went one after the other through VectorE, TensorE's sums, ScalarE and GpSimd, behind the second half's multiplications: GpSimd's four at 66.84 held a low half for which TensorE waits 5.50 us, VectorE's four at 68.50 the accumulations for which it waits 6.37. The sums of the last block stood behind fifteen slow products (5.19 us of idle VectorE), and these behind that wait and at the low clock (0.60 from 80 to 90 us). I had counted throughput and not this chain.

**The change of halves: forecast 4.7, measured 1.0; the second half 28.0 us, forecast 31.0.** Rival 2 was right in this: the second half's norm and features were worked off within the first half. It paid back 6.7 us, out of what the first half had lost to it. The sum closes: 114.4 + 14.7 + 12.2 - 6.7 - 1.0 for table products that found idle time is 133.6, measured 133.5.

**Behind the mark: "I take the delay at zero" failed too, 11.9 us.** I priced only the sums on TensorE, and rival 4 only those. What came is a jam in VectorE's list. Before, the query norm's root and the sweeps begin 8 and 7 us ahead of the mark (101.29 and 102.13 against 109.0); in the changed kernel they begin behind it (133.93 and 139.62 against 133.5), and so fall among the key norm, the multiplications that empty the banks of block 21 and the z blocks, and `te` and `to`, which lay behind the mark already. About half is the sweep arithmetic (e7, e8), 4 us is its lateness (e10); these two need not add. Low halves on VectorE instead of GpSimd are worth 3 to 4 us once the rest is mended (e15, e18). That these were the starved 14.72 us is not shown: in e14 and e17, on which e15 and e18 build, no low half behind the mark took more than 4.37 and 5.75 us. Which single order would do it alone stays open: each edit (e9, e13, e16) handed the wait to the next instruction in the list, and only the gate, the early tiles and the low halves together, on the mended opening, brought the stage back to 78.9 us (e18).

**What the signs said.** No transposes of x, and accumulations slow beside GpSimd: as written. First product near 20 us: 26.97. Last latent product near 113: 132.0. A hole near 81 us before the second half: TensorE does wait there, 6.37 us before 85.50, but within the first half; before the second half's first product it waits 1.01 us. The last sentence of the prediction, that a gain or loss that is not at the mark lies with the sweeps, pointed at the second loss; its price was bounded at 8 us without a row for VectorE's list.
